# Gated linear attention in a hybrid decoder layer: its 79 steps begun at turn 2 instead of turn 8, and issued 60 to the hundred turns instead of 56

## The chip, the cores and the metric

One core of a Trainium2 chip runs the whole layer. The metric is the device time of one launch in microseconds; the kernel before took 2313.78 us, the median of three runs from 2313.0 to 2314.23 us. Engines are named as in the profile: PE is TensorE, PEld its weight loads, DVE is VectorE, ACT is ScalarE, POOL is GpSimd, SP is SyncE, which here issues nearly all DMAs.

## What is computed

One decoder layer on 2048 tokens of width 1024, all in fp32. After an RMSNorm, one projection gives the inputs of two mixers. Their outputs are joined, projected by `w_out` and added to the input; an MLP of width 4096 with a squared ReLU and a last RMSNorm follow.

```python
proj = einsum('bsd,dp->bsp', rmsnorm(x, attn_norm_g), w_in)
gq, gk, gv, gr, glow, dq, dk_, dv_ = split(proj)
o_a = gla_mixer(gq, gk, gv, log_sigmoid(glow @ w2 + b) / 16)      # 4 heads
o_a = o_a * rsqrt(mean(o_a * o_a) + eps) * gla_norm_g * silu(gr)
o_b = dilated_mixer(dq, dk_, dv_, rel_bias)                       # 8 heads
h = x + concat([o_a, o_b]) @ w_out
h = h + square(relu(rmsnorm(h) @ w_ff1)) @ w_ff2
out = rmsnorm(h)
```

The gated linear attention (GLA, `gla_mixer`) carries a state from one block of tokens to the next: `S_t = diag(alpha_t) S_(t-1) + k_t v_t`, `o_t = q_t S_t`. The dilated attention (`dilated_mixer`) has three branches, with windows and strides (128, 1), (512, 4) and (2048, 16), each with a bias by distance and a softmax; the branches are combined by their denominators.

## The kernel before

The kernel has four stages that follow one another on PE: the input projection (up to about 533 us in the profile), the two mixers (533 to 884 us), the output projection with the second norm (to about 1100 us), and the MLP. Only the second is touched.

**The attention.** The dilated attention is cut into 160 units, each of two or four query blocks of one head and branch. A turn `k` of the loop at the end of the mixers' stage emits three things interleaved: the scores of unit `k + 3` (`Unit.scores`, matmuls L744 and L746 into PSUM banks `ps_c`, then on DVE the bias with a running minimum, L756, and on ACT the exponential, L757), the transposes of unit `k` (`Unit.transpose`, PE L766 into `ps_d`, copied to `pt` by ACT L773 or DVE L775 in turns), and the value products of unit `k - 2` (`Unit.values`, PE L785 into `ps_a`, copied out by DVE L788). Units come by pairs of heads: 40 for each of the four pairs. The last pair ends with the two heads' undilated branches side by side.

**What else the turns carry.** A dictionary `plan` holds further work by turn: `pack_q` (POOL L698, the queries of a strided branch gathered), `load_head` and `load_v` (DMAs), `combine_load` and `combine` (the three branches of a pair of heads; eight steps, on POOL for pairs 0 to 2, of which L843 and L845 are the long ones; shared by POOL and DVE for the last pair), and from turn 132, one in three turns, `load_wo`: one of eight pieces of the output projection's weights is loaded and split by ACT L986 and DVE L987 into two parts.

**GLA.** `gla_steps` is a generator of 79 steps over 16 tiles of 128 tokens. For tile `t` there are five, of which one already belongs to the next tile:

1. `gla_decay(t + 1)`: PE L912 into the one bank `ps_o`, two exponentials on ACT (L913, L914), and four or five products on POOL (L918, L920, L915).
2. the output of tile `t`: 16 matmuls, L945 and L946, into `ps_o`; ACT copies them (L947) and squares them (L949).
3. two transposes (L955) and a copy on ACT (L956); here the loads for tiles `t + 2` and `t + 1` are issued on SP (`gla_load`, `gla_load_v`, L897 to L905).
4. `gla_scores(t + 1)`: four matmuls, L925, into `ps_o`, which need POOL's products L915 and L918; DVE copies them under the causal mask (L926). Then the norm of the output of tile `t` (POOL L962, ACT L964) and its store, six turns later.
5. the state: four matmuls, L970, into `ps_o`, added to the state on DVE (L973) and scaled on ACT (L975).

The first two of the 79 steps are the decay and the scores of tile 0. All of them need the bank `ps_o` in turn. A turn issues one step or none:

```python
        if k >= G0 and (k - G0) * GE // 100 > (k - G0 - 1) * GE // 100:
            next(gla, None)
```

With `G0 = 8` and `GE = 56`, step `n` (from 0) stands at turn `8 + ceil(100 n / 56)`: the first at turn 8, and the last matmuls of GLA, the output of tile 15 (step 77), at turn 146.

**The order on the engines** is not the order of the text. The whole is built in a context with `schedule_with_timeline_sim=True`: a planner orders the instructions of each engine when the program is built, from its own idea of durations, and the order of the text gives the priority among what it takes to be ready. Only the beginning of the first stage stands under `tc.manual_schedule`, and single instructions are held by `tc.keep_in_program_order`. On the chip each engine then works through its instructions in the planned order and waits at the first whose inputs are not there.

Of the kernel before, what the change touches and what calls it, by code (L numbers as in the profile page):

```python
# [30 lines left out]
AHEAD, LAG = 3, 2  # L31

OTHER = [7, 9, 10, 11, 12, 13] + [14 * k + n for k in (1, 2, 3) for n in (0, 6, 10, 11, 12, 13)]
G0, GE = 8, 56
RELOAD = (10, 11, 12)
BANKS = {"a": 2, "c": 3, "d": 2, "o": 1}

# [1492 lines left out]
```

## Time and profile before

| | |
|---|---|
| median of three runs | 2313.78 us |
| the profiled execution's own time | 2312.57 us |
| its span, first to last instruction | 2310.8 us |
| PE busy, share of the span | 2282.6 us, 99% |
| mean granted TensorE clock | 0.995 |

The profile shows one execution. An engine is busy while it works; a row of a view gives a line of the kernel, the tile written and read, and in square brackets the idle time before it and what ended it. The granted clock is the share of TensorE's full clock that it was given. In views of stretches, each engine's busy time in that stretch stands beside its count of instructions.

### The profile page before, as it was taken

What the parts mean: (1) busy time and instruction counts of PE and PEld (TensorE: products, weight loads), DVE (VectorE), ACT (ScalarE), POOL (GpSimd) and SP (SyncE); (2) the same over time, 40 slices, a digit from 0 to 9 for tenths busy, and PEclk for the clock granted to TensorE, in tenths of its full rate; (3) what the DMA queues carried; (4) which work ended last, traced back from release to release, by engine and by line L of the source; (5) the groups of instructions that cost most, each with busy time, mean ns of one, the idle gap of its engine ahead of it and who ended that gap; (6) DMA issues with size and microseconds to landing.
All of it is one profiled execution on the core that took longest, in us unless ns stands there. A gap on an engine that the chain in (4) does not pass through costs nothing.

```text
span 2310.8 us, 34890 instructions
## 1 busy us (share of the span) xinstructions
PE 2282.6 (99%) x12652; PEld 1975.6 (85%) x12652; DVE 1550.3 (67%) x2863; ACT 1179.3 (51%) x2368; POOL 307.7 (13%) x394
## 2 busy tenths in 40 slices
PE   8999999999999999999999999999999999999998
PEld 7977998799999998888888888888888888888887
DVE  8887778766667676346877788777755346447444
ACT  5574546435877873235555566555543323225224
POOL 1120002025385672000000000000000100000002
PEclk9999999999999999999999999999999999999999
DMA  4457854786668864678644447444486477447553
GB/s 165 144 183 230 250 161 125 215 254 229 209 203 249 253 218 143 210 244 279 208 153 151 151 163 265 151 151 150 150 278 238 155 280 251 148 166 279 188 170 109
DMA packets 341805, 457.59 MB, mean 198 GB/s; under 512 B 18118, under 2 KB 214231, under 8 KB 336257
## 3 DMA queue, kind: packets, MB, share of 16 engines
q1 hardware_dynamic: 336878, 446.71, 59.3%
q10 hardware_dynamic: 4754, 8.66, 1.0%
q8 instruction: 99, 1.62, 0.3%
q14 instruction: 74, 0.60, 0.1%
HBM read 292.99 MB, written 167.02 MB: 199 GB/s over the span
## 4 chain that ended last, share of the span: by engine, by line
PE 51%; ACT 1%; DMA 0%; DVE 0%; issue 0%; DVEq 0%; ACTq 0%
PE ps_c L64 6%; PE ps_c L65 6%; PE ps_c L66 6%; PE ps_a L65 4%; PE ps_a L66 4%; PE ps_d L65 4%; PE ps_d L64 4%; PE ps_a L64 4%; PE ps_d L66 4%; PE ps_o L65 2%; PE ps_o L66 2%; PE ps_o L64 2%; DMA w1raw<-w_ff 0%; ACT scr L1355 0%; DVE hb L369 0%; ACT hb L368 0%
## 5 line engine op out<-in xcount | busy, mean ns | idle before, releaser
L369 DVE TENSOR_TENSOR ca<-ra,ca 128x1024 fp32r<-128x1024 f32 x112 | 138.0, 1233 | 161.6 <-ACT ca L368 161.6
L368 ACT ACTIVATE ca<-ra 128x1024 fp32r<-128x1024 f32 x112 | 118.0, 1053 | 221.3 <-PE ps_c L66 184.3
L368 ACT ACTIVATE w1comb<-w1raw 128x512 fp32r<-128x512 f32 x224 | 140.0, 627 | 153.7 <-PE ps_c L66 55.7
L1357 POOL TENSOR_TENSOR suma<-suma,gs 128x512 f32<-128x512 f32 x16 | 23.4, 1475 | 1393.7 <-ACT scr L1355 1393.7
L369 DVE TENSOR_TENSOR w1comb<-w1raw,w1comb 128x512 fp32r<-128x512 f32 x224 | 153.9, 689 | 51.8 <-ACT w1comb L368 51.7
L785 PE MATMUL ps_a<-v,pt 128*128 128x65 f32 x1200 | 178.2, 252 | 2.5 <-ACT pt L773 1.8
L785 PEld LDWEIGHTS ps_a<-v,pt 128*128 128x128 f32 x1200 | 175.1, 195 | 3.5 <-ACT pt L773 2.1
L757 ACT ACTIVATE pe<-pe,O 128x256 f32<-128x256 f32 (+1 forms) x384 | 156.6, 453 | 39.4 <-DVE O L756 36.1
L766 PE MATMUL ps_d<-ident,pe 128*128 128x128 f32 x600 | 159.9, 279 | 0.0
L756 DVE CUSTOM_DVE_ANT_0 pe<-ps_c,nb 128x256 f32<-128x256 f32 (+1 forms) x384 | 126.9, 361 | 39.6 <-PE ps_d L766 18.4
L207 ACT ACTIVATE wcomb<-wraw 128x512 fp32r<-128x512 f32 (+2 forms) x126 | 97.2, 773 | 88.7 <-PE ps_o L65 22.6
L368 ACT ACTIVATE cb<-rb 128x1024 fp32r<-128x1024 f32 x56 | 59.4, 1060 | 159.3 <-PE ps_o L65 98.8
L66 PE MATMUL ps_c<-cb,ca 128*128 128x512 f32 x336 | 130.7, 389 | 0.0
L66 PE MATMUL ps_c<-hb,w1comb 128*128 128x512 f32 x336 | 130.7, 389 | 0.0
L65 PE MATMUL ps_c<-cb,ca 128*128 128x512 f32 x336 | 130.7, 389 | 0.0
L64 PE MATMUL ps_c<-hb,w1comb 128*128 128x512 f32 x336 | 130.7, 389 | 0.0
L65 PE MATMUL ps_c<-hb,w1comb 128*128 128x512 f32 x336 | 130.7, 389 | 0.0
L64 PE MATMUL ps_c<-cb,ca 128*128 128x512 f32 x336 | 130.7, 389 | 0.0
L766 PEld LDWEIGHTS ps_d<-ident,pe 128*128 128x128 f32 x600 | 110.1, 187 | 0.1
L369 DVE TENSOR_TENSOR cb<-rb,cb 128x1024 fp32r<-128x1024 f32 x56 | 68.3, 1222 | 62.0 <-ACT cb L368 62.0
L1219 ACT ACTIVATE acc<-acc 128x512 f32<-128x512 f32 x128 | 79.6, 631 | 51.5 <-DVE acc L1239 35.8
L64 PE MATMUL ps_a<-wo,mT 128*128 128x512 f32 x256 | 101.3, 396 | 0.0
(419 smaller groups left out, 7038.9 us busy)
## 6 DMA issues: line engine op xcount, KB each, us to landing
ra<-actD SPq DMA_DIRECT2D x56, 1024.0 KB, 6.9
actD<-acc SPq DMA_DIRECT2D x192, 256.0 KB, 2.3
rb<-w_ff SPq DMA_DIRECT2D x72, 512.0 KB, 4.8
w1raw<-w_ff SPq DMA_DIRECT2D x32, 1024.0 KB, 6.2
k<-kD SPq DMA_DIRECT2D x16, 1024.0 KB, 7.9
rb<-hTD SPq DMA_DIRECT2D x13, 1024.0 KB, 7.1
wraw<-w_in SPq DMA_DIRECT2D x48, 256.0 KB, 3.7
cmb<-boD SPq DMA_DIRECT2D x16, 528.0 KB, 7.0
```

The source lines that it names most:

```text
L64: T.matmul(out, sh, mh, start=first, stop=False)
L65: T.matmul(out, sl, mh, start=False, stop=False)
L66: T.matmul(out, sh, ml, start=False, stop=last)
L207: A.activation(hi, src, AF.Copy, scale=sc)
L368: A.activation(hi, src, AF.Copy)
L369: V.tensor_tensor(lo, src, hi.bitcast(F32), op=OP.subtract)
L756: V.tensor_tensor_reduce(p, s, bias, scale=1.0, scalar=BIG, op0=OP.add, op1=OP.min, accum_out=nm)
L757: A.activation(p, p, AF.Exp, bias=nm, scale=-1.0)
L766: T.transpose(pb[:, i * 128:i * 128 + 128], src, ident)
L785: T.matmul(self.b.opsum[:, n % 4], self.pt[:, i * 128:i * 128 + 128], self.b.v[:, blk, cols], start=first, stop=last)
L1219: A.activation(v, v, AF.Relu)
L1357: G.tensor_tensor(C[0], C[0], gF[:, :512], op=OP.mult)
```

## The change

Two constants. Step `n` of GLA then stands at turn `2 + ceil(100 n / 60)`: the first at turn 2, the output of tile 15 at turn 131. Nothing is added and nothing left out; each of the 79 steps keeps its instructions, its DMAs and its place behind the attention of its turn.

```diff
-G0, GE = 8, 56
+G0, GE = 2, 60
```

## Prediction

> **What bounds the kernel now.** The page comes first: is there an engine that leaves nothing to gain?
>
> ```profile
> span 2310.8 us, 34890 instructions
> ...
> PE 2282.6 (99%) x12652; PEld 1975.6 (85%) x12652; DVE 1550.3 (67%) x2863; ACT 1179.3 (51%) x2368; POOL 307.7 (13%) x394
> ```
>
> PE is busy for all but 28.2 us of the span, and the change neither adds nor removes a matmul. It can only change how long PE waits, and only where GLA runs. So the next view is the waits of PE within the mixers' stage, 533 to 884 us (what waited, for what, us in total, times, longest):
>
> ```profile
> PE ps_o L925 <- POOL gla L915: 1.9, 1, 1.9
> PE ps_a L785 <- ACT pt L773: 1.8, 1, 1.8
> PE ps_a L785 <- DVE pt L775: 0.7, 1, 0.7
> PE ps_c L744 <- DVE O L756: 0.6, 1, 0.6
> ```
>
> That is all: 5.0 us in four waits. Where they lie, and what they cost beside themselves, the view of stretches tells (stretch, length, busy time and count of PE, PEld, DVE, ACT, POOL, then the granted clock, DMA share and rate):
>
> ```profile
> 533.00:832.00 299.00, 298.37 (x2677) 295.23 (x2675) 210.69 (x917) 233.04 (x692) 182.80 (x263) 1.00 0.72 226
> 832.00:884.00 52.00, 47.55 (x396) 45.91 (x394) 43.72 (x131) 40.20 (x111) 35.45 (x49) 0.93 0.76 240
> 836.50:841.10 4.60, 2.70 (x25) 2.43 (x23) 4.14 (x16) 3.13 (x8) 4.45 (x6) 1.00 0.45 172
> 841.10:844.50 3.40, 3.40 (x17) 3.31 (x16) 3.37 (x7) 1.15 (x4) 3.40 (x3) 0.50 0.59 161
> 844.50:867.00 22.50, 22.50 (x210) 22.24 (x209) 17.70 (x61) 18.82 (x52) 12.93 (x23) 1.00 0.95 293
> 871.80:875.20 3.40, 3.28 (x18) 3.28 (x19) 3.32 (x10) 1.95 (x5) 0.00 (x0) 0.50 0.90 293
> ```
>
> For 299 us PE is busy for 298.37, and the weight loads, whose ends are not modelled, for 295.23: nothing is to be had there. The last 52 us are another matter. PE is idle for 52 − 47.55 = 4.45 us, and twice a stretch of 3.40 us ran at half the clock, right after the waits of 1.9 and 1.8 us. Half the clock for 3.40 us costs 1.7 us. So the tail gives away 4.45 + 2 × 1.7 = 7.85 us, and that is the most that the change could bring here. DVE, 43.72 of 52 us (84%), is the next engine in it.
>
> **A rule against the row.** In the rows a wait of 1.9 us was enough for the clock to fall. The Trainium skill, page "TensorE: Matmul & The Clock Gate", Part 1, lets the clock halve after at least one idle window of about 3.4 us and asks for no idle gap above that. By that rule a removed wait of 1.9 us would be worth 1.9 us alone; by the rows it is worth 1.9 + 1.7 = 3.6 us, and the rows decide. The 3.4 us for which the low clock lasts is the page's window, and there the trace agrees.
>
> **The first wait** is GLA's own. POOL before it, and the instructions of ACT that it needed:
>
> ```profile
> 828.40 0.37 ACT L914 ACTIVATE gla<-ps_o 128x256 f32<-128x256 f32 x1
> ```
> ```profile
> 830.75 5.03 POOL L843 TENSOR_TENSOR cmb<-cmb,small 128x512 f32<-128x512 f32 x4
> 835.74 1.28 POOL L845 TENSOR_TENSOR O<-O,cmb 128x512 f32<-128x512 f32 x1
> 836.98 2.31 POOL L918 TENSOR_TENSOR gla<-gla 64x256 f32<-64x256 f32 x2
> 839.37 0.20 POOL L920 TENSOR_TENSOR gla<-gla 128x2 f32<-128x2 f32 x1
> 839.52 0.73 POOL L915 TENSOR_TENSOR gla<-gla 128x256 f32<-128x256 f32 x1
> ```
>
> The decay of tile 14 was ready on ACT at 828.77, and POOL took its products up at 836.98: for 8.2 us they stood behind the combining of pair 2. The scores of tile 14 (L925) stood on PE for them. In the text that decay is step 67, at turn 8 + 120 = 128 before and 2 + 112 = 114 after; the combining of pair 2 on POOL is issued from turn 124 to 138. After the change the decay precedes it, and this wait should go. Tile 15's decay moves from turn 137 to 122, before the combining too.
>
> **The second wait** is mixed:
>
> ```profile
> 866.39 1.34 DVE L987 TENSOR_TENSOR wo<-woraw,wo 128x1024 fp32r<-128x1024 f32 x1 [1.66 <-DMA mx<-mixD]
> 866.66 1.26 ACT L964 ACTIVATE gla<-gla,stats 128x128 f32<-128x128 f32 x4
> 868.23 1.04 ACT L986 ACTIVATE wo<-woraw 128x1024 fp32r<-128x1024 f32 x1
> 869.17 0.57 ACT L773 ACTIVATE pt<-ps_d 128x512 f32<-128x512 f32 x1
> 869.80 0.44 PE L785 MATMUL ps_a<-v,pt 128*128 128x65 f32 x2 [1.84 <-ACT pt L773]
> ```
>
> PE waited for a copy (L773) that stood in ACT's queue behind the norm of GLA's tile 14 (L964, 1.26 us) and a split of the output weights (L986, 1.04 us). The norm would leave; the split and DVE's wait of 1.66 us for its load would not. I leave this wait in, and take its going as a rival.
>
> **What moves, and whether it moves at all.** GLA in the trace does not stand at its turns:
>
> ```profile
> L766 PE MATMUL ps_d<-ident,pe x600: 269/278/417, 536.7 to 879.1; 128*128 128x128 f32 x150
> ```
> ```profile
> L912 PE MATMUL ps_o<-gla x64: 271/275/329, 534.8 to 851.2; 128*128 128x130 f32 x64
> L945 PE MATMUL ps_o<-gla x128: 269/275/328, 557.9 to 877.7; 128*128 128x128 f32 x128
> ```
>
> L766 belongs to turns 0 to 159, so a turn takes (879.1 − 536.7) / 159 = 2.15 us, and turn 8 begins at 554. The first decay (L912) ran at 534.8: the planner took it as soon as its loads allowed, and beginning at turn 2 can hardly bring it forward. The last output (L945, turn 146, 851 us) ended at 877.7, some twelve turns late. A tile took (851.2 − 534.8) / 15 = 21.1 us; at 56 steps to the hundred turns it should take 5 / 0.56 × 2.15 = 19.2, at 60 it would be 17.9. So the chain was slower than its turns already, held by its own links and by POOL, and a faster rate helps only in so far as priority against POOL's other work holds it. The last output moves by 15 turns in the text, 32 us; I let it move by about half.
>
> How much PE work thereby leaves the tail? GLA's instructions in it alone, by engine in the same columns, and then two rows of DVE's groups by line:
>
> ```profile
> 832.00:884.00 52.00, 9.68 (x56) 7.48 (x56) 3.61 (x9) 13.89 (x51) 14.79 (x23) 0.93 0.76 240
> ```
> ```profile
> L973 DVE TENSOR_TENSOR gla<-gla,ps_o 64x256 f32<-64x256 f32 x4 | 1.7, 417 | 0.5 <-PE ps_o L970 0.5
> L926 DVE COPY_PREDICATED gla<-gla,ps_o 128x512 f32<-128x512 int32 x2 | 1.4, 721 | 0.0
> ```
>
> On PE between 7.48 us (weight loads) and 9.68 us (matmuls, which overlap): I take 8.5. Half is 4.25 us, which is then paid between 533 and 832 us in full, since PE has no idle time there. On DVE only 1.7 + 1.4 = 3.1 us are GLA's (the rest of the 3.61 is combining in the same tile); half is 1.55.
>
> **The sum.** Without half of GLA the tail holds, on PE, 52 − 7.85 − 4.25 = 39.9 us, and on DVE 43.72 − 1.55 = 42.2 us: DVE becomes the longer. How well can it be kept busy? At 84%, as now, the tail takes 42.2 / 0.84 = 50.2 us, at 100% it takes 42.2. Half-way, 92%, gives 45.9. With the 4.25 us paid earlier that is 50.1 against 52: 1.9 us less; the ends are 54.5 (2.5 more) and 46.4 (5.6 less). The middle also agrees with the first wait gone (3.6 less) and 1.7 us given back to DVE.
>
> The other parts I set at nothing, each with its cover. GLA's loads on SP come earlier with their step:
>
> ```profile
> SPq L904 <- PE ps_o L970: 23.2, 6, 6.3
> ```
> ```profile
> gla<-gvD SPq DMA_DIRECT2D x14, 256.0 KB, 3.9
> ```
>
> They land in 3.9 us and are issued a tile ahead, 21.1 us; without that cover they would cost 3.9 us once. SP stood before one of them up to 6.3 us until a state matmul had released its buffer, and behind it on SP are loads of keys, queries and output weights; these waits move with GLA, out of the part where output weights are loaded. POOL's packing and combining now queue behind GLA's products, which take 1.44 + 0.20 + 0.73 = 2.4 us a tile where nothing disturbs them:
>
> ```profile
> 603.58 1.44 POOL L918 TENSOR_TENSOR gla<-gla 64x256 f32<-64x256 f32 x2 [11.17 <-ACT gla L913]
> 605.09 0.20 POOL L920 TENSOR_TENSOR gla<-gla 128x2 f32<-128x2 f32 x1
> 605.24 0.73 POOL L915 TENSOR_TENSOR gla<-gla 128x256 f32<-128x256 f32 x1
> ```
>
> POOL has 299 − 182.80 = 116 us free ahead of the tail, which hides that. If a packed query came late to its scores, PE would wait: bound 0 below and 2.4 + 1.7 = 4.1 us above, and I take nothing, as no such wait is among the four of before.
>
> The profiled execution took 2312.57 us, 1.77 around its span, and lies 1.2 us under the median of the runs; the difference is applied to the median: 2313.78 − 1.9 = 2311.9 us.
>
> **Rivals.** *Both waits go.* The tail gives back all of 7.85 us: 2305.9. For it: both have GLA in the queue ahead of them. Against: DVE would have to do its 42 to 44 us with hardly a gap, and the weights' loads stay. 14%.
>
> *Nothing moves.* The chain keeps its place because its links and not its turns hold it: 2313.8, with the waits as they are. For it: the first decay ran 19 us ahead of its turn, and a tile took 21.1 us where the rate allowed 19.2. Against: the 8.2 us behind the combining is a matter of order, and the order changes. This is also the case that the change doesn't do what it says. 20%.
>
> *Slower: the tail without GLA is DVE's.* If all 8.5 us of GLA leave the tail, they are paid earlier in full, and the tail must shrink to 52 − 8.5 = 43.5 us to break even. DVE still has 43.72 − 3.1 = 40.6 us in it (scores' bias, copies, weight splits, combining of the last pair), so it would have to be busy for 93% of it; GLA's matmuls were what PE did while DVE caught up. At the 84% of now the tail takes 48.3, and the whole 48.3 + 8.5 − 52 = 4.8 us more: 2318.6. For it: DVE at 3.37 of 3.40 and 3.32 of 3.40 us right after both waits. Against: from 844.5 to 867 DVE was busy for 17.70 of 22.50 with PE full. 20%.
>
> *Half moves, the forecast*: 46%, with its own range of 2308.2 to 2316.3.
>
> **The numbers.** A measurement of this kernel tells a change of about 0.2%, 4.6 us, from none: faster is below 2309.2, slower above 2318.4. Faster: the rival with both waits gone, 14%, and 1.0 of the 8.1 us of the forecast's range, 6% : 20%. Slower: most of the DVE rival, 16%. The rest, 64%, within. The range goes from 2306.0, the rival with both waits gone, to 2318.6, the DVE rival; about half of each of the two lies outside, under 20% together.
>
> **What would show it.** In the changed profile: the scores of tile 14 (L925) without idle time before them, and its products on POOL before the combining of pair 2; the last L945 some 16 us before 877.7; PE as full as before between 533 and 832 us; DVE's share of the last 50 us before the final L785 at 90% or more, with PE's waits now for DVE (L756, L775). Each stretch at clock 0.50 counts 1.7 us. Wrong would be: the last output still near 877 us (nothing moved), a new wait of PE ahead of 832 us for a packed query or a load, or a tail that loses its two waits and gets none in their place.

## The result

The two kernels, measured side by side on the same chip:

| | before | after |
|---|---|---|
| median (lowest to highest, runs) | 2313.39 us (2312.56 to 2315.14, 6) | 2329.95 us (2329.26 to 2334.06, 6) |
| ratio, 95% interval | | 1.0075 [1.0062, 1.0088] |
| profiled execution, its span | 2312.57 us, 2310.8 us | 2329.26 us, 2327.5 us |

The change made the kernel 16.6 us slower. That is above the range of the prediction, 2306.0 to 2318.6 us, and above its slower rival too. The page of the changed kernel, first the engines over the whole span:

```profile
span 2327.5 us, 34912 instructions
...
PE 2286.4 (98%) x12652; PEld 1976.0 (85%) x12652; DVE 1554.4 (67%) x2863; ACT 1180.8 (51%) x2368; POOL 303.4 (13%) x394
```

The same 12652 matmuls, with 2327.5 − 2286.4 = 41.1 us in which PE is idle, against 28.2 before. Where is PE waiting now? The waits of PE from 533 to 915 us, a little beyond the mixers' stage, in the columns of the prediction (what waited, for what, us in total, times, longest), the four longest:

```profile
PE ps_d L393 <- POOL O L845: 9.5, 1, 9.5
PE ps_a L785 <- DVE pt L775: 3.2, 1, 3.2
PE ps_c L393 <- DMA mx<-mixD: 2.9, 2, 2.0
PE ps_c L744 <- DVE O L756: 0.6, 1, 0.6
```

The wait for POOL L915 is gone, and in its place stands the longest wait of the two profiles. L393 is a transpose at the beginning of the output projection, and its input `O` is the combined attention that POOL L845 adds up. It lies behind the stretch that the prediction looked at. The view of stretches shows that (stretch, length, busy time of PE, PEld, DVE, ACT, POOL, clock, DMA share, rate); after first, then the third of these stretches in the kernel before:

```profile
533.00:832.00 299.00, 298.37 (x2675) 295.00 (x2674) 207.27 (x910) 233.23 (x696) 169.39 (x241) 1.00 0.71 225
832.00:884.00 52.00, 46.47 (x394) 44.16 (x393) 45.91 (x136) 38.94 (x105) 27.87 (x44) 0.97 0.66 205
884.00:912.00 28.00, 16.01 (x59) 12.15 (x59) 16.52 (x27) 2.61 (x6) 22.70 (x32) 0.70 0.34 114
891.10:908.20 17.10, 7.14 (x21) 5.23 (x22) 8.53 (x13) 1.91 (x4) 14.56 (x23) 0.50 0.16 47
```
```profile
884.00:912.00 28.00, 28.00 (x137) 23.26 (x137) 15.11 (x29) 5.40 (x13) 4.85 (x5) 1.00 0.38 120
```

From 884 to 912 us PE was full before. Now it is idle for 28 − 16.01 = 11.99 us, and the clock stood at 0.50 for 17.1 us, in which PE was busy for 7.14 us: at the full clock that would take about half, so by this estimate 3.57 us are lost on top. POOL, which had 4.85 us of work here, now has 22.70: work that came late. Between 832 and 884 us the loss is 5.53 us of idle time and 1.7 us for one stretch of 3.4 us at half clock, 7.23 where it was 7.85. Together 7.23 + 11.99 + 3.57 = 22.8 us against 7.85, which is 14.9 of the 16.7 us between the two spans. The other 1.8 us have no row of their own.

**Why is POOL late?** POOL's own queue in the changed kernel, around the combining of pair 2 (start, length, what, and in brackets the idle time before it):

```profile
815.71 0.40 POOL L825 TENSOR_TENSOR gla<-gla,cmb 128x16 f32<-128x16 f32 x2
822.26 1.44 POOL L918 TENSOR_TENSOR gla<-gla 64x256 f32<-64x256 f32 x2 [6.15 <-ACT gla L913]
...
845.94 1.44 POOL L918 TENSOR_TENSOR gla<-gla 64x256 f32<-64x256 f32 x2 [12.97 <-ACT gla L913]
...
859.14 2.05 POOL L843 TENSOR_TENSOR O<-O,small 128x512 f32<-128x512 f32 x2
...
880.80 2.49 POOL L843 TENSOR_TENSOR O<-O,gla 128x512 f32<-128x512 f32 x2
883.26 4.07 POOL L843 TENSOR_TENSOR cmb<-cmb,gla 128x512 f32<-128x512 f32 x4
...
887.84 2.52 POOL L845 TENSOR_TENSOR O<-O,cmb 128x512 f32<-128x512 f32 x2
890.32 1.04 POOL L843 TENSOR_TENSOR O<-O,small 128x512 f32<-128x512 f32 x1
...
900.79 1.26 POOL L845 TENSOR_TENSOR O<-O,cmb 128x512 f32<-128x512 f32 x1
```

POOL was not short of time; it stood idle for 6 and 13 us in front of GLA's products. The differences of pair 2's second half (L825) were done at 816.1 us, but the long products (L843) of the first half began at 859.14 and those of the second at 880.80 us. Pair 3's first products ran into them, and the sums of the two ended at 902.05 us; PE's 9.5 us end there. Between the differences and the products lies one instruction on ACT, the exponential L828. Its place in ACT's queue, after, then before:

```profile
854.23 0.30 ACT L949 ACTIVATE gla<-gla 128x128 f32<-128x128 f32 x1
854.43 0.19 ACT L949 ACTIVATION_READ_ACCUMULATOR gla<-gla 128x1 f32 x1
854.52 0.23 ACT L828 ACTIVATE small<-small 128x48 f32<-128x48 f32 x1
...
865.79 0.31 ACT L949 ACTIVATE gla<-gla 128x128 f32<-128x128 f32 x1
866.00 0.19 ACT L949 ACTIVATION_READ_ACCUMULATOR gla<-gla 128x1 f32 x1
866.10 0.23 ACT L828 ACTIVATE gla<-gla 128x48 f32<-128x48 f32 x1
```
```profile
803.70 0.49 ACT L757 ACTIVATE pe<-pe,O 128x256 f32<-128x256 f32 x1
804.10 0.23 ACT L828 ACTIVATE small<-small 128x48 f32<-128x48 f32 x1
...
816.10 0.23 ACT L828 ACTIVATE gla<-gla 128x48 f32<-128x48 f32 x1
```

After the change the two exponentials follow, each time, directly upon the last square of an output step of GLA (L949), and both come 50 us later than before. The code says why:

```python
        tc.keep_in_program_order(A.activation(E, E, AF.Exp))      # L828
```

This hold ties the exponential to the ACT instruction that stands before it in the text. For pair 2 the two are issued at the beginning of turns 125 and 132, so what stands before them is the end of turns 124 and 131. There, behind the attention, comes GLA's step, if the turn has one. With (8, 56) neither turn has one, and the hold falls upon an instruction of the attention, which runs at its turn. With (2, 60) step 73, the output of tile 14, stands at 2 + ceil(7300 / 60) = 124, and step 77, the output of tile 15, at 131. But GLA runs far behind its turns. At 2.15 us a turn, 124 and 131 begin at about 803 and 818 us, and these outputs ended at 854 and 866. The exponentials, their products on POOL and all that queues behind them went along.

### The profile page after: what moved, and what is told of

Same layout as the page of the kernel before. It is cut to its first block, busy times and chain, and to the rows that moved or that the text cites. A ratio compares the mean times of both kernels' runs of the same rounds, so it can differ in the third digit from the quotient of the medians.

```text
span 2327.5 us, 34912 instructions
## 1 busy us (share of the span) xinstructions
PE 2286.4 (98%) x12652; PEld 1976.0 (85%) x12652; DVE 1554.4 (67%) x2863; ACT 1180.8 (51%) x2368; POOL 303.4 (13%) x394
## 4 chain that ended last, share of the span: by engine, by line
PE 93%; DVE 4%; ACT 1%; DMA 1%; issue 1%; POOL 0%; DVEq 0%; ACTq 0%
PE ps_a L65 10%; PE ps_a L66 10%; PE ps_a L64 10%; PE ps_c L64 8%; PE ps_c L65 8%; PE ps_c L66 8%; PE ps_d L64 4%; PE ps_d L66 4%; PE ps_d L65 4%; PE ps_a L785 4%; PE ps_o L64 4%; PE ps_o L65 4%; PE ps_o L66 4%; PE ps_d L766 3%; PE ps_c L744 2%; PE ps_c L746 2%
## 5 line engine op out<-in xcount | busy, mean ns | idle before, releaser
L369 DVE TENSOR_TENSOR ca<-ra,ca 128x1024 fp32r<-128x1024 f32 x112 | 138.0, 1232 | 167.8 <-ACT ca L368 167.8
L369 DVE TENSOR_TENSOR w1comb<-w1raw,w1comb 128x512 fp32r<-128x512 f32 x224 | 153.8, 688 | 54.5 <-ACT w1comb L368 53.6
L369 DVE TENSOR_TENSOR cb<-rb,cb 128x1024 fp32r<-128x1024 f32 x56 | 68.3, 1221 | 64.3 <-ACT cb L368 64.1
```

The costliest lines, as they stand in the source:

```text
L369: V.tensor_tensor(lo, src, hi.bitcast(F32), op=OP.subtract)
```

## The experiments

Three theories stood at the beginning. **P**: the hold does it, as just told. **Q**: GLA, earlier in the text, has priority over the combining on POOL and pushes it back. **R**: the tail is DVE's, as the prediction's slower rival had it. Two further letters stand in expectations. **S**: what is left without the hold is chance, of the order that the planner gives each text. **T**: the place of GLA's step in its turn, and not the hold, makes the difference between 2330 and 2316 us. In the expectation of the last run, Q means something else: that run only asks whether a further gain comes. Times are medians with their lowest and highest; each ratio is to the kernel before on the same chip. It took 2313.39, 2313.44, 2313.14 and 2313.65 us in the four sets of runs, so times of different chips can be set side by side to about half a us.

**Taking the hold away.** In the changed kernel:

```diff
-        tc.keep_in_program_order(A.activation(E, E, AF.Exp))
+        A.activation(E, E, AF.Exp)
```

> The changed kernel, with the exponential of the combining no longer held in program order on ACT. Theory P (the hold): with the first step at turn 2 and 60 to the hundred, the turn before each exponential of pair 2's combining ends with a GLA output step (tiles 14 and 15), and the hold ties the exponentials (L828) behind its squares (L949), at 854.5 and 866.1 us; freed, they run near 805 and 818 us, the wait of PE for the combined O at 902 us goes, and the time falls to 2307 to 2316 us. Theory Q (POOL's priority): GLA's products stand ahead of the combining on POOL because their turns are now earlier, and POOL waits at them; freeing an instruction of ACT changes little, 2325 to 2332 us. Theory R (DVE is the bound of the tail): no change either, 2325 to 2332 us.

2316.81 us (2315.68 to 2322.54, 10 runs), 1.0018 [1.0008, 1.0027]. 13.1 of the 16.6 us are gone. ACT's queue shows the exponential at once:

```profile
803.18 0.23 ACT L828 ACTIVATE small<-small 128x48 f32<-128x48 f32 x1
```

**Keeping the hold, but moving GLA ahead of the attention in the text of its turn,** so that the end of each turn is the attention's:

```diff
+        if k >= G0 and (k - G0) * GE // 100 > (k - G0 - 1) * GE // 100:
+            next(gla, None)
         alternate(pv, sc, tr)
-        if k >= G0 and (k - G0) * GE // 100 > (k - G0 - 1) * GE // 100:
-            next(gla, None)
```

> The changed kernel, with all holds left in, but GLA's step of a turn traced ahead of the turn's attention instead of behind it; the last instruction of ACT and DVE before the next turn's combining is then one of the attention. Theory P: the holds fall on instructions that run at their turn, L828 of pair 2 near 805 and 818 us, time 2307 to 2316 us. Theory Q: GLA stands ahead of POOL's other work as before or more so, 2325 to 2332 us. Theory R: 2325 to 2332 us.

2316.12 us (2313.39 to 2319.01, 10), 1.0012 [1.0002, 1.0021]. The exponentials ran at 804.41 and 818.33 us. This gives GLA more priority, not less, and most of the loss goes all the same: Q would have it stay, and so would R. The waits of PE in this kernel:

```profile
PE ps_a L785 <- DVE pt L775: 3.2, 2, 2.9
PE ps_a L785 <- ACT pt L773: 1.6, 1, 1.6
PE ps_c L744 <- DVE O L756: 1.1, 1, 1.1
```

The wait in the output projection has vanished. What is left is in the prediction's tail.

**The two constants one by one.** `G0, GE = 2, 56`:

> The start alone: first step at turn 2, 56 to the hundred as before the change. Theory P: pair 2's exponentials stand behind the output of tile 13 and the decay of tile 15, so they come at about 830 and 846 us, 20 to 30 us late instead of 50; time 2314 to 2324 us. Theory Q: the decay of tile 15 moves from turn 137 to 131, 6 of the 15 turns; time 2317 to 2322 us. Theory R: GLA leaves the tail by less; 2315 to 2322 us.

2324.33 us (2322.65 to 2324.66, 4), 1.0046 [1.0031, 1.0061]. With these numbers the turns 124 and 131 end with steps 68 and 72, the output of tile 13 and the decay of tile 15, which lag as well, though not so far:

```profile
834.25 0.19 ACT L949 ACTIVATION_READ_ACCUMULATOR gla<-gla 128x1 f32 x1
834.34 0.23 ACT L828 ACTIVATE small<-small 128x48 f32<-128x48 f32 x1
...
847.95 0.37 ACT L914 ACTIVATE gla<-ps_o 128x256 f32<-128x256 f32 x1
848.21 0.24 ACT L828 ACTIVATE gla<-gla 128x48 f32<-128x48 f32 x1
```

PE's longest waits there lie in the output projection too: 4.4 us for a split on DVE (L369), which stood behind DVE's part of pair 3's combining, and 3.2 us for POOL's L845.

And `G0, GE = 8, 60`:

> The rate alone: first step at turn 8 as before the change, 60 to the hundred. Theory P: pair 2's exponentials stand behind attention, and only the reciprocal of its first half behind the norm of tile 13; time 2309 to 2317 us, near the kernel before. Theory Q: 9 of the 15 turns, 2321 to 2326 us. Theory R: 2318 to 2326 us.

2314.09 us (2311.89 to 2316.73, 10), 1.0002 [0.9992, 1.0011]: no step falls on turn 124 or 131 (the steps around them stand at 123, 125, 130 and 132), the exponentials ran at 809.3 and 823.0 us, and nothing is lost. So the four settings line up by the time of the two exponentials: 804 and 816 us, 2313.4; 809 and 823, 2314.1; 834 and 848, 2324.3; 854 and 866, 2330.0. The first 5 to 7 us cost nothing; 30 us and more do, once the combining no longer ends before it is needed.

**Putting the hold back by itself.** In the kernel with GLA ahead of the attention, pair 2's exponentials alone are ordered behind the last square of GLA traced so far, with no other change:

```diff
+        if pr == 2:
+            tc.add_manual_dep(ins.ins, gst["last"].ins.name, mybir.DependencyInfo(
+                mybir.DependencyClass.NoSync, mybir.DependencyReason.DATA), reason="hold")
...
-                A.activation(gst["sq"], o[:, h], AF.Square, accum_out=ss[:, h:h + 1])
+                gst["last"] = A.activation(gst["sq"], o[:, h], AF.Square, accum_out=ss[:, h:h + 1])
```

> GLA traced ahead of the attention (first step at turn 2, 60 to the hundred, 2316.1 us), with one thing put back: pair 2's two exponentials are ordered behind the last square traced before them, those of tiles 14 and 15, as the hold did in the changed kernel. Nothing else differs, and ordering is all that is added. Theory P: L828 of pair 2 comes near 855 and 866 us again, PE waits for the combined O, 2326 to 2333 us. Theory T (the place of GLA's step in the turn made the fall from 2330 to 2316 us, not the hold): 2313 to 2319 us.

2327.7 us (2326.85 to 2330.87, 5), 1.0062 [1.0050, 1.0075]. The exponentials came at 853.89 and 865.78 us, and with them the wait (the added lines shift the numbers behind them by 3, so L848 is L845 here):

```profile
PE ps_d L393 <- POOL O L848: 8.3, 1, 8.3
PE ps_c L393 <- DMA mx<-mixD: 3.8, 2, 2.4
```

From 2316.1 to 2327.7 us by the hold alone: P is shown from both sides, by taking the hold out and by putting it in, and T falls.

**Late combining without GLA's part.** In the kernel before, the hold taken away as above and pair 2's combining moved back by 24 turns:

```diff
+                        late = 24 if pr == 3 else 0
-                        combine_at(pr - 1, 8 * half, 8, first - 2 + 7 * half, [first + 4 + 7 * half + n for n in range(8)])
+                        combine_at(pr - 1, 8 * half, 8, first - 2 + 7 * half, [first + 4 + late + 7 * half + n for n in range(8)])
```

> The kernel before (first step at turn 8, 56 to the hundred), with the combining's exponential free and the eight steps of each half of pair 2's combining issued 24 turns later, so that they run about 51 us late, as they did in the changed kernel. Theory P (a late combining of pair 2 alone makes the time): POOL works it off after the attention's end, pair 3's combining stands behind it, PE waits for the combined O (L393 behind L845) 6 to 12 us at half clock; 2323 to 2333 us. Theory Q (GLA's place on POOL makes it): GLA stands as in the kernel before, so the time stays at 2311 to 2316 us.

2334.01 us (2331.77 to 2335.2, 4), 1.0090 [1.0075, 1.0105]. In this kernel pair 2's last steps come between those of pair 3, with which they share the small tile of weights, so part of the two combinations is computed with other weights; the amount of work is the same. PE waited 17.2 us, for a load of `mx` rather than for L845: the combined blocks of pair 2 go through HBM, and here their way back was the last to arrive (stores of `mixD` issued at 897.5 us, the loads behind them at 901.7, PE went on at 904.4). With 19 turns in place of 24 the two do not mix:

> The kernel before with the combining's exponential free, and the eight steps of each half of pair 2's combining issued 19 turns later (40.9 us), so that they end just ahead of pair 3's. Theory P: pair 2's long products on POOL run at 850 to 890 us instead of 819 to 849, and pair 3's behind them; PE waits for combined or stored O; 2319 to 2331 us. Theory Q (GLA's place on POOL): as before, 2311 to 2316 us.

2337.85 us (2335.01 to 2339.47, 4), 1.0102 [1.0088, 1.0115]. That is more than expected:

```profile
PE ps_d L393 <- POOL O L845: 11.6, 1, 11.6
PE ps_c L393 <- DMA mx<-mixD: 5.3, 1, 5.3
PE ps_a L785 <- DVE pt L775: 4.1, 1, 4.1
```

A late combining is thus enough by itself, with GLA where it was, and the same wait comes of it. It costs 8 us more than in the changed kernel, though the exponentials came at 858.0 and 860.6 us, about the same time. Here all eight steps of each half move back, the first differences too, and PE waits longer for both the sum and the loads; how the 8 us divide stays open.

**Does GLA follow its turns at all?** GLA ahead of the attention, and `G0, GE = 0, 100`: a step in every turn, the last matmuls at turn 77.

> GLA traced ahead of the attention, one step in every turn from turn 0: the last matmuls of GLA stand at turn 77, far ahead. It shows how fast the chain can go by its own links. If turns held it, the last output (L945) comes near 705 us; if its links hold it (a tile about 19 us, as between tiles 7 and 13 of the kernel before), it comes after 840 us. Time: theory P with the holds out of the way 2311 to 2320 us; theory Q, GLA ahead of all combining on POOL, 2325 us or more.

2316.89 us (2314.35 to 2319.45, 10), 1.0017 [1.0007, 1.0026]. GLA's decays and outputs, first and last start:

```profile
L912 PE MATMUL ps_o<-gla x64: 272/275/329, 535.2 to 845.1; 128*128 128x130 f32 x64
```
```profile
L945 PE MATMUL ps_o<-gla x128: 271/275/418, 557.2 to 869.7; 128*128 128x128 f32 x128
```

The text let it end 54 turns earlier than in the changed kernel, and its last output started at 869.7 us. A tile took (845.1 − 535.2) / 15 = 20.7 us, against 21.1 before: its turns are not what holds GLA. Whether the links of its own chain do, or the places that the planner gives its matmuls among the others on a full PE, this run does not tell apart. The same priority taken to its end costs POOL's other work nothing that shows: Q falls. And GLA ahead in the kernel before, with (8, 56):

> The kernel before, with GLA's step of a turn traced ahead of the attention. Theory P: in the kernel before the holds of pair 2's exponentials fall on the attention already, so this takes nothing away in the tail: 2310 to 2316 us. Theory Q: no change either, 2311 to 2316 us. It tells whether tracing GLA ahead is worth anything by itself, so that the fall from 2330 us to 2316 us is the holds' and not the order's.

2314.35 us (2313.02 to 2316.63, 10), 1.0005 [0.9995, 1.0014]; its last output started at 869.1 us. Once the holds fall upon the attention, (8, 56), (2, 60) and (0, 100) give 2314.4, 2316.1 and 2316.9 us, with intervals that overlap: the constants are then worth 2.5 us at most.

**What is left: DVE?** Freed of the hold the change still costs 2.7 to 3.4 us. In both such kernels PE waits 3.7 or 2.9 us, at 874 us, for a copy that DVE makes (L775). So in the last 22 turns all these copies go to ACT, on top of GLA ahead:

```diff
-            if turn[0]:
+            if turn[0] or clock[0] >= NU - 22:
```

> GLA's step traced ahead of the attention in its turn, first step at turn 2 and 60 to the hundred, and in the last 22 turns all copies of transposed probabilities go to ACT (L773), none to DVE (L775). Theory R (what is left over 2313.4 us once the holds are out of the way is DVE's, which the tail without GLA keeps waiting): some 10 copies of 0.68 us leave DVE, the wait of PE for L775 near 874 us goes with its half clock, time 2309 to 2313 us. Theory S (what is left is chance of the planned order): time stays at 2314 to 2318 us or gets worse.

2310.47 us (2308.95 to 2317.28, 10), 0.9992 [0.9983, 1.0002]. The stretch of the tail with GLA ahead, and the same with the copies on ACT:

```profile
832.00:884.00 52.00, 46.05 (x386) 43.54 (x385) 46.95 (x133) 38.72 (x107) 34.23 (x47) 0.97 0.77 243
```
```profile
832.00:884.00 52.00, 46.83 (x399) 44.14 (x399) 40.49 (x127) 42.78 (x114) 38.04 (x54) 1.00 0.75 236
```

DVE goes from 46.95 to 40.49 us, ACT from 38.72 to 42.78, the clock stays at 1.00, and the median falls by 5.6 us, with a range that overlaps. That speaks for R as to the remainder. The same copies on ACT in the kernel before:

> The kernel before with all copies of transposed probabilities of the last 22 turns on ACT. Theory R (DVE binds the tail): the waits near 870 us go in part, 2307 to 2312 us. Theory S (chance of the planned order): 2311 to 2317 us.

2314.46 us (2310.46 to 2317.08, 11), 1.0000 [0.9991, 1.0008]: nothing, where R expected 2307 to 2312 us, although DVE had 37.13 us left in the tail and no stretch at half clock remained there. And with `G0, GE = 8, 60`, GLA ahead and the copies on ACT:

> First step at turn 8, 60 to the hundred, GLA traced ahead of the attention, and the copies of the last 22 turns on ACT. Since GLA's turns do not move GLA and the holds fall on attention, theory P expects the same as with the first step at turn 2: 2309 to 2312 us. Theory Q expects a gain over that, 2304 to 2309 us.

2312.21 us (2308.5 to 2316.71, 11), 0.9989 [0.9980, 0.9998]. It lies 0.1% under the kernel before, which is hardly more than can be measured. Whether the 2.7 to 3.4 us belong to DVE, or to the order that the planner happens to give each text, these runs do not settle.

## Why the prediction was wrong

**Right: where PE can lose nothing.** From 533 to 832 us PE is busy for 298.37 us, to the hundredth what it was, and no packed query came late.

**Right: the first wait goes.** L925 no longer waits for POOL. But the decay's earlier turn was not needed for it: with the turns of before and the combining moved back by 19 or 24 turns this wait is gone as well, for nothing then stands in front of GLA's products. In the changed kernel the long products of pair 2 had been held back to 859 us. Nor is it worth its 3.6 us by itself: the kernels with GLA ahead, (0, 100) among them, lose this wait too and gain nothing.

**Right in size, and by luck: the last output moves by 14.6 us.** It was foreseen to move by 16:

```profile
L945 PE MATMUL ps_o<-gla x128: 272/275/347, 557.1 to 863.1; 128*128 128x128 f32 x128
```

877.7 − 863.1 = 14.6 us. But the turns do not explain it. With the turns of before the last output started at 862.4 us (combining 24 turns late), 863.1 (19 turns late), 869.1 (GLA ahead) and 873.4 (copies on ACT); with a step in every turn at 869.7. A POOL without the combining thus moves it as far by itself, and that is the likelier reason here too; no run shows it for the changed kernel.

**Wrong, though the time did not hang on it: half of GLA does not leave the tail.** "Half is 4.25 us", says the sum of PE's work. GLA's instructions in the tail after the change, in the columns of the prediction's row:

```profile
832.00:884.00 52.00, 9.20 (x54) 7.23 (x54) 4.04 (x9) 11.32 (x41) 11.32 (x18) 0.97 0.66 205
```

PE has 9.20 us of GLA there where it had 9.68: of 56 matmuls 54 are still in the tail, and 0.48 us left it, not 4.25. In the changed kernel without the hold it is 9.55 us, with a step in every turn 11.16. The last output now starts 31 us behind 832 us instead of 46, so hardly any work crossed that line. In every profile of this case PE has 9.0 to 11.2 us of GLA in the tail; the case that the slower rival describes, a tail without GLA, never came about.

**Right in kind, not for its reason: PE waits for DVE in the tail.** PE's largest wait in it is for DVE's L775, 3.2 us, and DVE is busy for 45.91 of 52 us, 88%, where 90% or more was named as the sign. The sum let DVE become the longer engine because PE's work shrinks; PE's work stayed, and DVE's rose from 43.72 us. Both waits of before went, the second too, which the sum had left in: 1.9 + 1.8 + 2 × 1.7 = 7.1 us. Yet the tail lost 7.23 us where it had lost 7.85, for nearly all came back, 3.2 + 1.7 = 4.9 us of it with the wait for L775 and its stretch at half clock. Of the 1.9 us that the sum gains, 0.6 came in the tail.

**The step that made the time wrong** is "The other parts I set at nothing", in its sentence on POOL: "POOL's packing and combining now queue behind GLA's products", hidden by the 116 us that POOL has free. It asked whether POOL had time, and POOL had. What the combining needed was ACT's exponential, L828, and the cost of moving GLA's turns past that instruction was never put down. The bound taken there, 4.1 us for a packed query, was of another wait; the combining had no bound at all. The runs showed 11 to 13 us in its place: 2329.95 − 2316.81 = 13.1 us with the hold taken out, 2327.70 − 2316.12 = 11.6 us with it put in. The two facts that would have told it stood there: `combine` has its hold in the code, and GLA was seen to run "some twelve turns late". An instruction tied to a stream that lags will lag with it; and after the change the output of tile 14 ended (854 − 803) / 2.15, some 24 turns behind its own.

The list of what would make the prediction wrong looked for a new wait "ahead of 832 us". It came at 892 to 902, in the next stage. For the same reason the slower rival, DVE's tail, had the right sign and not the cause: freed of the hold, the changed kernel lies at 2316 to 2317 us, near that rival's 2318.6, but with GLA's work still in the tail; and the change as made is 11 us beyond it.

## What to carry to other kernels

A hold such as "keep this in program order" ties an instruction to whatever happens to be traced before it. When a stream that runs late is given other turns, look up for each hold which instruction now stands in front of it, and when that one really runs; two constants can move it from the attention to the slowest chain of the kernel. Ask of work that is "hidden by free time" also what it waits for on other engines, and follow it as far as its reader, in the next stage if need be. And when work is said to leave a stretch, count what of it is still there.

## What the runs showed of the hardware

**Short waits and the clock.** From the mixers' stage on the clock fell in these runs to 0.50 after every idle time of PE of 1.84 us or more, mostly for 3.4 us. Between 1.6 and 1.8 us it could go either way: it fell after 1.67 us (the kernel before with GLA ahead) and 1.74 us (start alone), and stayed after 1.71 and 1.75 us (GLA ahead; 19 turns late). Below that, 1.61 us and less, it stayed. With the long waits of the output projection it was low for 10.2 to 23.9 us, in steps of about 3.4. The page "TensorE: Matmul & The Clock Gate" of the Trainium skill, Part 1, calls the window of about 3.4 us free-running. That fits the steps, and it may be why gaps of one length went both ways; its rule of an idle gap above 3.4 us does not fit these falls.

**Small DVE instructions beside POOL.** While POOL ran the late sums, of 1.26 us each (2.52 us for two at 887.84, shown above), DVE's small products on pair 3's weights were stretched:

```profile
887.48 0.17 DVE L832 TENSOR_TENSOR gla<-gla 128x8 f32<-128x8 f32 x1
887.68 0.22 DVE L831 TENSOR_TENSOR gla<-gla,cmb 128x8 f32<-128x8 f32 x1
887.94 1.22 DVE L832 TENSOR_TENSOR gla<-gla 128x8 f32<-128x8 f32 x1
```

The same instruction takes 0.17 us and then 1.22, about the length of one of POOL's. The Trainium skill, page "SBUF — State Buffer", section "Who interferes with whom", has the two engines share a pair of ports by an exclusive lock, and the row agrees: the small one waits the large one out. Combining that comes late thus also slows the DVE work that it meets; how much of the lost time that makes, no run shows.
